# Output projection of the last 14 token tiles: pairs of tiles by seven block products in place of eight

## The chip, the core and the metric

The kernel runs on one core of one Trainium2 chip. TensorE (PE) multiplies, VectorE (DVE), ScalarE (ACT) and GpSimd (POOL) do elementwise work, and the SyncE queue (SP) issues the DMA transfers. The metric is device microseconds for one launch, as a median of runs; the kernel before took 1576.73 us (three runs, 1571.05 to 1579.54).

## The reference

One layer of a hybrid backbone is applied to 128 context tokens and 2048 latent tokens of width 1024. What matters here is the end of the layer:

```
ya = ya.astype(x.dtype) * jax.nn.silu(g_a)
yb = b_gate * _short_conv(c_gate * u_conv, ...) * jax.nn.silu(g_b)
u = jnp.concatenate([ya, yb], axis=-1) @ lp['w_out']        # (tokens x 1024) @ (1024 x 1024)
return x + gate * u, s_final                                # then _rmsnorm(.., final_g)
```

`ya` (channels 0 to 511) comes out of a bidirectional RWKV-7 scan and is the last to be ready; `yb` (channels 512 to 1023) comes out of a short convolution and is ready long before. The output is normalised per token and scaled by `final_g`.

## The kernel before

Phase 1 (to about half of the span) makes the projections and the operands of the scan and spills them to scratch memory. Phase 2 (`phase2`, line 828) runs 17 stages of the scan, each with its masked Gram products (`Gm`, `Fm`, `Qm`), an inverse on GpSimd (`I`, L1103 and L1106), the operators (`E`, L1201, evicted by `Ev`, L1206), the states (`S`, L1232, handed on by `sv`, L1258), the outputs (`y`, L1277 and L1279), and an ending per block of 512 tokens that normalises, gates and stores the mixed channels to scratch (`fw fr fq fm T fy fa`, L1298 to L1339). Stage 15 is the context, stage 16 the last latent block.

Phase 3 (`phase3`, line 1460) is the output projection, mixed into the end of phase 2. It takes 17 tiles of 128 tokens in the order `TILES` (5 to 12, 0, 13 to 16, 1 to 4). Everything is float32 made of two fp32r parts: a high part (a copy on ScalarE) and a low part (the difference, on VectorE). A product of two such numbers is three matmuls: high by high, high by low, low by high. Per tile:

- `cL`, `aL` (or `AL`) load the four conv channel groups and the four scan channel groups of the tile (L1495, 256 KB each); `cH`, `aH` make the high part (L1502, ScalarE), `cD`, `aD` the low part (L1508, VectorE).
- `P` and `B` (L1515 to L1517) are the conv half and the scan half of the product, for each of the two column halves of 512: 4 groups x 3 matmuls = 12 matmuls of 128x512 each, so 48 matmuls per tile and 816 in all. For tiles 5, 6 and 7 (`AHEAD`) the conv half is made ahead (`AP`) and parked by ScalarE (`AE`, L1529).
- `Z` multiplies the sum in PSUM by the gate on VectorE (L1574; with a parked half L1571 and L1572), `G` adds x on GpSimd (L1580; on VectorE for the last tile), `Q` squares and sums on ScalarE (L1588), `ss rt rc` make the inverse root (L1592, L1595, L1598), `fo` scales on VectorE and stores (L1603, L1604), `xL` loads x (L1548).
- The weights are loaded and split once: `CL CH CD` (conv groups, low part on VectorE) and `WL WH WD` (scan groups, low part on GpSimd), L1480 to L1489.

From stage 13 on the order of the work is a list written out by hand, `LATE` (line 778): one word per step, `name@tile` or `name@stage`, run by `main` (line 1398) inside `tc.manual_schedule` for PE, VectorE and ScalarE. The instructions of these three engines stand in the order of the list. GpSimd and the SP queue are ordered by the program's scheduler. `R` opens the first memory of phase 3 (`begin`), `Lo` the rest (`begin_left`, which also loads the gate rows and `final_g`).

Of the kernel before, what the change touches and what calls it, by code (L numbers as in the profile page):

```python
# [827 lines left out]
def phase2(K):  # L828
# [457 lines left out]
    def finish(p, blk, y):  # L1286
# [32 lines left out]
        q = tl([128, 512], "w", 1)  # L1319
# [78 lines left out]
    def main():  # L1398
# [4 lines left out]
        order = tc.manual_schedule(engines={mybir.EngineType.PE, mybir.EngineType.DVE, mybir.EngineType.Activation})  # L1403
# [5 lines left out]
        for word in LATE.split():  # L1409
            n, t = word.split("@")  # L1410
            if n == "R":
                O.pm.close()
                O.r2.close()
                O.r1.close()
                K.last["R"]()
                K.body = NST
            elif n == "Lo":
                for p in (O.p2, O.l1):
                    p.close()
                K.last["Lo"]()  # L1420
            elif "." in t:
# [38 lines left out]
def phase3(K):  # L1460
# [4 lines left out]
    wk, raws, mts, pss, z0, zs, xs, sss = {}, {}, {}, {}, {}, {}, {}, {}  # L1465
    CONV, ATT = (4, 5, 6, 7), (0, 1, 2, 3)
    TILES = [5, 6, 7, 8, 9, 10, 11, 12, 0, 13, 14, 15, 16, 1, 2, 3, 4]
    AHEAD = TILES[:3]
    HALF = [slice(0, 512), slice(512, 1024)]

    def begin():
# [4 lines left out]
        z0[AHEAD[0]] = O.r.tile([128, 1024], F32, name="z0_0")  # L1476
# [42 lines left out]
    def ahead(h):  # L1519
        def f(i):  # L1520
            ps = pss[h, i] = O.pr.tile([128, 512], F32, tag="u", name=f"psa{i}_{h}")
            products(ps, mts["c", i], HALF[h], CONV, True, True)
        return f

    def ahead_out(h):
        def f(i):
            if i not in z0:
                z0[i] = K.spare(5 + len(z0), f"z0_{i}", F32)
            P.copy(z0[i][:, HALF[h]], pss.pop((h, i))[:])  # L1529
# [5 lines left out]
    def begin_left():  # L1535
        O.l = Pool(K, "p3l", "left")
# [40 lines left out]
    def added(h):  # L1577
        def f(i):
            cs = HALF[h]
            (V if i == TILES[-1] else G).tensor_tensor(zs[i][:, cs], zs[i][:, cs], xs[i][:, cs], ALU.add)  # L1580
# [19 lines left out]
    def out(i):  # L1600
        z = zs.pop(i)
        for cs in HALF if i == TILES[-1] else [slice(0, 1024)]:
            V.scalar_tensor_tensor(z[:, cs], z[:, cs], sss[i][:, 0:1], O.fg[:, cs], ALU.mult, ALU.mult)  # L1603
            D(S["y"][i * 128:i * 128 + 128, cs], z[:, cs])  # L1604
# [56 lines left out]
```

## Time and profile before

| | |
|---|---|
| median of 3 runs | 1576.73 us |
| profiled execution | 1576.59 us |
| its span (first to last instruction) | 1574.8 us, granted clock 0.986 |
| busy PE, VectorE, ScalarE, GpSimd | 1491.7, 1158.8, 773.0, 666.4 us |
| 816 products of the output projection | 1364 to 1567 us |

Times in the profile count from the first instruction. The page gives shares over the whole span; this change touches only the end, so the windows from about 1316 us on are read. "Busy" of PE counts pipelined matmuls that overlap; the distance between the starts of two matmuls tells what one costs.

### The profile page before, as it was taken

To read this page: it belongs to the slowest core of one execution; us is meant where nothing else is said; L and a number is where in the kernel's file an instruction comes from. 1 tells how busy PE (TensorE), PEld (TensorE's weight loads), DVE (VectorE), ACT (ScalarE), POOL (GpSimd) and SP (SyncE) were. 2 spreads that over 40 slices of the span, in tenths; PEclk is the share of its full clock that TensorE was granted. 3 is DMA by queue.
4 is the path that set the end of the run, shared out by engine and by line. 5 is a ranking of instruction groups with operands and counts; after the bars stand their busy time and mean duration, and the time that the engine had idled before them with its cause. 6 is when DMAs were issued, how large, how long until landed. Compare 5 with 4: busy or idle time off the path is not lost.

```text
span 1574.8 us, 39408 instructions
## 1 busy us (share of the span) xinstructions
PE 1491.7 (95%) x16180; PEld 1382.8 (88%) x16180; DVE 1158.8 (74%) x1959; ACT 773.0 (49%) x1464; POOL 666.4 (42%) x1026
## 2 busy tenths in 40 slices
PE   5899999999999999999999999999999897899998
PEld 3899989999999999999999997888888786678786
DVE  5999995673999847569995447798998997645533
ACT  4566652342555314136541117887878776523222
POOL 0133330000333572933323605888888887122121
PEclk9999999999999999999999998999999999999999
DMA  9669998653877765538987537566676754636442
GB/s 370 207 189 271 261 268 324 214 203 133 201 230 223 211 234 197 184 106 253 251 244 253 189 124 194 136 178 177 183 209 172 183 155 148 203 116 192 147 142 94
DMA packets 204580, 313.79 MB, mean 199 GB/s; under 512 B 58088, under 2 KB 147560, under 8 KB 190320
## 3 DMA queue, kind: packets, MB, share of 16 engines
q1 hardware_dynamic: 168816, 311.13, 63.3%
q10 hardware_dynamic: 35584, 0.14, 1.4%
q8 instruction: 127, 2.08, 0.6%
q14 instruction: 53, 0.43, 0.1%
HBM read 208.05 MB, written 103.17 MB: 198 GB/s over the span
## 4 chain that ended last, share of the span: by engine, by line
PE 63%; DVE 13%; DMA 8%; POOL 6%; issue 4%; ACT 2%; SPq 1%; ACTq 0%; DVEq 0%; POOLq 0%
PE psE L1201 4%; POOL zt L1106 4%; PE psu L1515 4%; PE psu L1516 4%; PE psu L1517 4%; PE psS L1232 2%; POOL ztmp L1103 2%; PE mmc L182 2%; PE mmc L184 2%; PE mmb L182 2%; PE mmc L183 2%; PE mmb L184 2%; PE mmb L183 2%; PE mmu L182 2%; PE mmu L184 2%
## 5 line engine op out<-in xcount | busy, mean ns | idle before, releaser
L1106 POOL TENSOR_TENSOR zt<-zt,ztmp 128x30 f32<-128x30 f32 (+7 forms) x510 | 213.7, 419 | 39.8
L1103 POOL TENSOR_TENSOR ztmp<-ab,zt 128x60 f32<-128x60 f32 (+7 forms) x255 | 142.2, 558 | 66.9 <-DVE ab L1094 45.4
L1232 PE MATMUL psS<-sv,E 128*64 128x64 f32 x2176 | 103.2, 229 | 13.6 <-DVE sv L1258 9.1
L1232 PEld LDWEIGHTS psS<-sv,E 128*64 128x64 f32 x2176 | 82.4, 138 | 37.8 <-issue 14.5
L410 POOL TENSOR_TENSOR sh<-rawl 128x384 f32<-128x384 f32 (+1 forms) x48 | 46.4, 983 | 151.5 <-ACT rawl L401 151.5
L1580 POOL TENSOR_TENSOR z<-z,x 128x512 f32<-128x512 f32 x32 | 42.7, 1338 | 151.3 <-DVE z L1574 85.9
L1206 DVE TENSOR_TENSOR E<-psE,msk 128x512 f32<-128x512 f32 x136 | 90.9, 684 | 20.8 <-PE psE L1201 19.9
L434 POOL TENSOR_TENSOR hsl<-sq,hsh 128x384 fp32r<-128x384 f32 (+1 forms) x24 | 32.5, 1356 | 129.9 <-ACT hsh L429 129.9
L1187 ACT ACTIVATE stf<-psX 64x512 f32<-64x512 f32 x136 | 80.3, 590 | 13.2 <-PE psX L1183 10.5
L1258 DVE TENSOR_TENSOR sv<-psS,pc 64x128 f32<-64x128 f32 x254 | 64.0, 273 | 22.4 <-PE psS L1232 21.8
L182 PE MATMUL mmg<-h,w 128*128 128x384 f32 (+1 forms) x216 | 70.8, 328 | 0.0
L183 PE MATMUL mmg<-h,w 128*128 128x384 f32 (+1 forms) x216 | 70.7, 327 | 0.0
L184 PE MATMUL mmg<-h,w 128*128 128x384 f32 (+1 forms) x216 | 70.6, 327 | 0.0
L182 PE MATMUL mmb<-h,w 128*128 128x384 f32 (+1 forms) x192 | 62.9, 328 | 5.4 <-ACT w L150 2.8
L184 PE MATMUL mmc<-h,w 128*128 128x384 f32 (+1 forms) x192 | 63.4, 330 | 0.9 <-DVE w L154 0.9
L182 PE MATMUL mmv<-h,w 128*128 128x384 f32 (+1 forms) x192 | 63.1, 328 | 1.1 <-DVE sg L524 1.1
L182 PE MATMUL mmc<-h,w 128*128 128x384 f32 (+1 forms) x192 | 63.5, 331 | 0.2 <-DMA w<-scr_wsp 0.2
L183 PE MATMUL mmc<-h,w 128*128 128x384 f32 (+1 forms) x192 | 63.3, 330 | 0.0
L182 PE MATMUL mmu<-h,w 128*128 128x384 f32 (+1 forms) x192 | 62.7, 326 | 0.0
L184 PE MATMUL mmv<-h,w 128*128 128x384 f32 (+1 forms) x192 | 62.6, 326 | 0.0
L183 PE MATMUL mmb<-h,w 128*128 128x384 f32 (+1 forms) x192 | 62.6, 326 | 0.0
L184 PE MATMUL mmb<-h,w 128*128 128x384 f32 (+1 forms) x192 | 62.6, 326 | 0.0
(316 smaller groups left out, 5069.9 us busy)
## 6 DMA issues: line engine op xcount, KB each, us to landing
w<-scr_wsp SPq DMA_DIRECT2D x68, 1024.0 KB, 6.1
scr_wsp<-w SPq DMA_DIRECT2D x34, 1024.0 KB, 5.2
rr<-scr_ops SPq DMA_DIRECT2D x32, 1024.0 KB, 7.7
scr_ops<-xs SPq DMA_DIRECT2D x160, 192.0 KB, 5.7
wr<-in_win SPq DMA_DIRECT2D x34, 512.0 KB, 8.8
x<-in_x SPq DMA_DIRECT2D x17, 512.0 KB, 3.2
wadas<-in_wada SPq DMA_DIRECT2D x8, 1024.0 KB, 13.6
sv<-scr_vt SPq DMA_DIRECT2D x32, 256.0 KB, 4.1
```

The costliest lines, as they stand in the source:

```text
L182: T.matmul(ps[:, :n], w[:, 0, k], hh[:, 0, k, :n], start=k == 0, stop=False)
L183: T.matmul(ps[:, :n], w[:, 0, k], hh[:, 1, k, :n], start=False, stop=False)
L184: T.matmul(ps[:, :n], w[:, 1, k], hh[:, 0, k, :n], start=False, stop=k == 7)
L1103: G.tensor_tensor(tv, ab[:, j:j + 2, j + 2:32].unsqueeze(1).broadcast_to((128, kn, 2, n)), zt[:, :kn, j:j + 2].unsqueeze(3).broadcast_to(( ...
L1106: G.tensor_tensor(zt[:, :kn, j + 2:32], zt[:, :kn, j + 2:32], tv[:, :, r], ALU.subtract)
L1187: P.activation(g.fs[64:128, :, hd, e::2], g.ps["X"][e][hr_].rearrange("p a (b t) -> p b a t", b=2), AF.Copy, scale=-1.0)
L1201: T.matmul(pe[r, i, hd, :].rearrange("p (b t) -> p b t", b=2), lt[:, b, hd, us.start + k + i], rt[:, :, hd, us.start + k + i], start=True, ...
L1206: V.tensor_tensor(g.E[n][:, k:k + 2].rearrange("p a b c -> p (a b) c"), pe[:].rearrange("p a b c -> p (a b) c"), B.msk[:, ME[g.d]].unsquee ...
L1232: T.matmul(g.sp[i // 4][r, q, hd, :], g.E[n][:, k, hd, r], g.sv[:, u, hd, :], start=True, stop=True)
L1258: V.tensor_tensor(dst, g.sp[i // 4][0:64, q], B.pc[0:64, d, 2 * p:2 * p + 2, c:c + 1].broadcast_to((64, 2, 64)), ALU.mult)
L1515: T.matmul(ps[:], mh[:, n], hi[:, cs], start=start and n == 0, stop=False)
L1516: T.matmul(ps[:], mh[:, n], lo[:, cs], start=False, stop=False)
```

## The change

The order list changes from `R@0` on, and a new word `Tl` at that point ends the ordered block and opens another that also holds GpSimd and SP: from there their instructions, the DMA issues too, stand in the order of the list.

Tiles 5, 6 and 7 (`SINGLE`) stay as they were, 48 matmuls each; the conv half made ahead is kept for tile 5 alone and is cut into words of three matmuls (`A10` and so on). The other 14 tiles go in seven pairs (`TWO`: 8 and 9, 10 and 11, 12 and 0, 13 and 14, 15 and 16, 1 and 2, 3 and 4). A pair is seen as a 2 x 2 block matrix: rows are the two tiles, columns the channel groups `K1` (0, 1, 4, 5) and `K2` (2, 3, 6, 7). The weight is seen as 2 x 2 blocks of `K1`, `K2` by the two column halves. In place of eight block products (96 matmuls) there are seven (`M1` to `M7`, 84 matmuls): four of them take sums of left blocks (`s1` to `s4`), four take sums of right blocks (`t1` to `t4`), and the results are put together by further additions (`EX E2 C11 E3 C22 E4 C12 C21`).

- Per pair: both tiles' mixed channels are loaded by two transfers of 512 KB (`mLa`, `mLb`); four left sums on VectorE (128x512); seven high parts on ScalarE (`H..`) and seven low parts on VectorE (`D..`) in place of four and four.
- Per pair the results: `EX` is a copy on ScalarE, `E2 E3 E4` one VectorE addition each (PSUM plus SBUF), `C11 C22 C12 C21` a VectorE addition and a multiplication by the gate each; before, there were four multiplications (`Z`).
- Once: the four weight groups of each half are loaded again (`vL`, three transfers, 1 MB, four times), 16 right sums on VectorE (`t`), 16 high parts on ScalarE (`tH`), 16 low parts on VectorE (`tD`). The fourth right block overwrites weights that only the single tiles use. The memory for the others is opened by `Lw`, after the last ending of phase 2.
- The additions of x (`G`) stay on GpSimd for 15 tiles; the last two tiles have them on VectorE.
- The last endings of phase 2 (block 0 of p 3) get memory of their own; the states of stage 16, which before lay between the products, come ahead of `Lo`, save the last of them.

```diff
-E010@14 zi@16 ... pre@16 I@16 E110@14 Ev100@14
 ...
-fm@11.1 n@15 Qm0@16 sv11@14 Qe0@16 X0@15 R@0 CL@5 CL@4 S21@14 Xc00@15 T@11.1 sv21@14 S31@14 fy@11.1 Xc10@15
+fm@11.1 n@15 Qm0@16 sv11@14 Qe0@16 X0@15 R@0 Tl@0 y11@13 S21@14 y00@14 CL@5 sv21@14 T@11.1 CL@4 S31@14
 ...
+Ev110@15 U@16 E111@15 WH@0 WL@1 t1@0 sv71@14 Ev111@15 bu@16 E101@15 Ev101@15 E000@15 vL@1 WD@0 E001@15
 ...
+T@14.1 E101@16 Ev001@16 WD@3 AL@5 E100@16 sv61@15 sv71@15 y11@15 fy@14.1 Ev100@16 S00@16 sv00@16 S01@16 WH@2
+sv01@16 E010@16 fa@14.1 S11@16 S10@16 AH@5 Ev010@16 sv10@16 fc@15.1 fw@15.1 AD@5 E011@16 S20@16 sv20@16
 ...
+sv41@16 S51@16 sv50@16 S60@16 A03@5 fy@15.1 Lo@0 aH@5 sv51@16 S61@16 sv60@16 aD@5 fa@15.1 AH@6 AE0@5 S70@16
 ...
+aH@6 fy@16.1 fa@16.1 Lw@0 tH1@0 aD@6 aL@7 Q1@5 tH2@0 P1r@6 tH1@1 AH@7 B0@6 B1@6 tD1@1 tD2@0 tD1@0 tH3@0
+tD3@0 vL@2 aH@7 AD@7 G0@5 tH3@1 Z0@6 aD@7 tD3@1 Z1@6 Q0@5 G0@6 t1@2 t3@2 tH2@1 P0s@7 t2@2 G1@6 ss@5 rt@5
+tH1@2 mLa@0 mLb@0 rc@5 fo@5 tD2@1 tD1@2 P1r@7 vL@3 Q1@6 Ha11@0 Da11@0 s3@0 s1@0 Hs3@0 Ha22@0 s2@0 B1@7 Hs1@0
 ...
+M4@6 rc@1 fo@1 C22@6 G0@3 Q0@3 E4@6 C12@6 G1@4 Q1@4 G1@3 C21@6 Q1@3 ss@3 G0@4 rt@3 rc@3 fo@3 Q0@4 ss@4 rt@4
+rc@4 fo@4
 ...
+            if n == "Tl":
+                order.__exit__(None, None, None)
+                order = tc.manual_schedule(engines={E.PE, E.DVE, E.Activation, E.Pool, E.SP})
+                order.__enter__()
 ...
-            (V if i == TILES[-1] else G).tensor_tensor(zs[i][:, cs], zs[i][:, cs], xs[i][:, cs], ALU.add)
+            (V if i in TILES[-2:] else G).tensor_tensor(zs[i][:, cs], zs[i][:, cs], xs[i][:, cs], ALU.add)
 ...
+    def right_sum(n):
+        def f(j):
+            o = right_raw(n, j)
+            x, y = {1: (right_raw(3, j), o), 3: (right_raw(2, j), o), 2: (o, right_raw(1, j)), 4: (o, right_raw(2, j))}[n]
+            V.tensor_tensor(o, x, y, ALU.subtract)
+        return f
 ...
+    def left_sum(n):
+        def f(q):
 ...
+            x, y, op = dict(s3=("a11", "s1", ALU.subtract), s1=("s1", "a22", ALU.add), s2=("a22", "s3", ALU.subtract),
+                            s4=("a12", "s2", ALU.subtract))[n]
+            V.tensor_tensor(left_raw(n, q), left_raw(x, q), left_raw(y, q), op)
+        return f
 ...
+    def seventh(n):
+        def f(q):
+            c, nm = (q * 7 + ORDER.index(n)) % 4, f"psw{n}_{q}"
+            ps = pss[n, q] = (O.pr if c == 1 else O.pl).tile([128, 512], F32, tag="u", name=nm) if c % 2 else K.bank(nm)
+            mh, ml = lw[LEFT[n], q]
+            for j in range(4):
+                hi, lo = right(n, j)
+                T.matmul(ps[:], mh[:, j], hi, start=j == 0, stop=False)
+                T.matmul(ps[:], mh[:, j], lo, start=False, stop=False)
+                T.matmul(ps[:], ml[:, j], hi, start=False, stop=j == 3)
+        return f
 ...
+    def plus(n, src, dst, gate=False):
+        def f(q):
+            z, gb = part(q, *dst)
+            V.tensor_tensor(z, pss[n, q][:], part(q, *src)[0], ALU.add)
+            if gate:
+                V.tensor_tensor(z, z, gb, ALU.mult)
+        return f
```

More of the change, by code (lines that the diff above doesn't have):

```diff
@@ L1420, in main @@
                 K.last["Lo"]()
+            elif n == "Lw":
+                O.l0.close()
+                K.last["Lw"]()
             elif "." in t:
@@ L1429, in main, with small, bank @@
         O.pS.close()
-        for p in (O.l0, O.rI, O.r0):
+        for p in (O.rI, O.r0):
             p.close()
-    K.early, K.main, K.spare = early, main, spare
+    def small(tag, name, dt=F32):
+        return (O.rI if tag in ("zt", "dg") else O.r0).tile([128, 512], dt, tag=tag, name=name, bufs=2 if tag == "zt" else 1)
+    def bank(name):
+        return O.pS.tile([128, 512], F32, tag="S", name=name)
+    K.early, K.main, K.spare, K.small, K.bank = early, main, spare, small, bank
 def layout2(I):
@@ L1517, in products, with ahead @@
             T.matmul(ps[:], ml[:, n], hi[:, cs], start=False, stop=stop and n == 3)
-    def ahead(h):
+    def ahead(h, n):
         def f(i):
-            ps = pss[h, i] = O.pr.tile([128, 512], F32, tag="u", name=f"psa{i}_{h}")
-            products(ps, mts["c", i], HALF[h], CONV, True, True)
+            if n == 0:
+                pss["a", h, i] = O.pr.tile([128, 512], F32, tag="u", name=f"psa{i}_{h}")
+            ps, (mh, ml), (hi, lo), cs = pss["a", h, i], mts["c", i], wk[CONV[n]], HALF[h]
+            T.matmul(ps[:], mh[:, n], hi[:, cs], start=n == 0, stop=False)
+            T.matmul(ps[:], mh[:, n], lo[:, cs], start=False, stop=False)
+            T.matmul(ps[:], ml[:, n], hi[:, cs], start=False, stop=n == 3)
         return f
@@ L1526, in f @@
         def f(i):
[L1527 to L1529 removed]
+            P.copy(z0[i][:, HALF[h]], pss.pop(("a", h, i))[:])
         return f
@@ L1535, in begin_left @@
     def begin_left():
-        O.l = Pool(K, "p3l", "left")
+        O.l = Pool(K, "p3l", "right")
         O.pl = Pool(K, "p3pl", "left", 2, PSUM)
@@ L1601, in out, with two_ways @@
         z = zs.pop(i)
-        for cs in HALF if i == TILES[-1] else [slice(0, 1024)]:
+        for cs in HALF if i in TILES[-2:] else [slice(0, 1024)]:
             V.scalar_tensor_tensor(z[:, cs], z[:, cs], sss[i][:, 0:1], O.fg[:, cs], ALU.mult, ALU.mult)
             D(S["y"][i * 128:i * 128 + 128, cs], z[:, cs])
+    def two_ways():
+        O.w = Pool(K, "p3w", "left")
+        for n in range(1, 4):
+            tw[n] = [[O.w.tile([128, 512], F32R, name=f"tw{n}{a}{j}") if (n, j, a) != (1, 0, "h") else K.small("dg", "tw1h0", F32R) for a in "hl"] for j in range(4)]
+        tw[4] = [[w[:, HALF[1]] for w in wk[k]] for k in K1]
@@ new lines, in again, with right_raw @@
+    def again(j):
+        vr = raws["v", j] = K.spare(6 + j % 2, f"wa{j}", F32), K.small("zt", f"wb{j}"), K.small(("Q00", "Q01", "Q10", "Q11")[j], f"wc{j}")
+        a, b = [slice(k * 128, k * 128 + 128) for k in (K1[j], K2[j])]
+        D(vr[0][:], A["wout"][a, :])
+        D(vr[1][:], A["wout"][b, HALF[1]])
+        D(vr[2][:], A["wout"][b, HALF[0]])
+    def right_raw(n, j):
+        ab, b22, b21 = raws["v", j]
+        return {1: ab[:, HALF[0]], 2: b22[:], 3: ab[:, HALF[1]], 4: b21[:]}[n]
@@ new lines, in part, with first_out, f @@
+    def part(q, r, h):
+        i = TWO[q][r]
+        return zs[i][:, HALF[h]], O.gb[:, 0 if i else 1, HALF[h]]
+    def first_out(q):
+        for t, i in zip((0, 1), TWO[q]):
+            zs[i] = K.spare(6 + t, f"zw{i}", F32) if q % 2 else tl([128, 1024], "z", i)
+        P.copy(part(q, 1, 0)[0], pss[1, q][:])
+    def plus(n, src, dst, gate=False):
+        def f(q):
+            z, gb = part(q, *dst)
+            V.tensor_tensor(z, pss[n, q][:], part(q, *src)[0], ALU.add)
+            if gate:
+                V.tensor_tensor(z, z, gb, ALU.mult)
+        return f
@@ L1613, in phase3 @@
     for h in range(2):
-        K.last.update({f"AP{h}": ahead(h), f"AE{h}": ahead_out(h), f"P{h}r": conv_part(h, "pr"), f"P{h}l": conv_part(h, "pl"),
+        K.last.update({f"A{h}{n}": ahead(h, n) for n in range(4)})
+        K.last.update({f"AE{h}": ahead_out(h), f"P{h}r": conv_part(h, "pr"), f"P{h}l": conv_part(h, "pl"), f"P{h}s": conv_part(h, "pS"),
                        f"B{h}": att_part(h), f"Z{h}": gated(h), f"G{h}": added(h), f"Q{h}": squares(h)})
+    for n in range(1, 5):
+        K.last.update({f"t{n}": right_sum(n), f"tH{n}": right_high(n), f"tD{n}": right_low(n), f"s{n}": left_sum(f"s{n}")})
+    for n in LEFT.values():
+        K.last.update({f"H{n}": left_high(n), f"D{n}": left_low(n)})
+    for n in range(1, 8):
+        K.last[f"M{n}"] = seventh(n)
+    K.last.update(EX=first_out, E2=plus(6, (1, 0), (0, 1)), C11=plus(2, (1, 0), (0, 0), True), E3=plus(7, (0, 1), (1, 0)),
+                  C22=plus(5, (1, 0), (1, 1), True), E4=plus(5, (0, 1), (0, 1)), C12=plus(3, (0, 1), (0, 1), True), C21=plus(4, (1, 0), (1, 0), True))
+    K.last.update(Lw=lambda _=0: two_ways(), vL=again, mLa=both_load(0), mLb=both_load(1))
 def layout3(I):
```

148 lines of the change are left out of this document (98 added, 50 removed).

## The prediction

> **What bounds the kernel now.** I first read the windows of the end, where the change lies: per stretch, busy time of PE, PEld, VectorE, ScalarE and GpSimd (instructions in brackets), granted clock, DMA share, GB/s.
>
> ```profile
> span 1574.8 us, 39408 instructions
> ...
> 1316.20:1364.20 48.00, 36.13 (x718) 30.49 (x717) 31.79 (x60) 31.77 (x50) 19.75 (x26) 0.93 0.56 167
> 1364.20:1405.40 41.20, 37.47 (x171) 29.40 (x169) 17.65 (x29) 11.32 (x25) 5.63 (x5) 0.92 0.51 158
> 1405.40:1449.00 43.60, 43.60 (x224) 34.71 (x223) 29.83 (x50) 11.59 (x31) 10.83 (x8) 1.00 0.54 176
> 1449.00:1567.40 118.40, 118.34 (x552) 95.25 (x550) 49.31 (x84) 29.86 (x73) 26.38 (x20) 1.00 0.40 135
> 1567.40:1574.80 7.40, 0.00 (x0) 0.00 (x0) 3.10 (x6) 1.02 (x3) 0.00 (x0) 0.63 0.20 72
> 1316.20:1574.80 258.60, 235.55 (x1657) 189.84 (x1656) 131.69 (x227) 85.56 (x180) 62.58 (x59) 0.96 0.47 149
> ```
>
> From 1405 to 1567 us TensorE never stops, and VectorE is free more than half of the time (118.4 - 49.3 us in the longest stretch). So the products set the end, and a product less is time won as long as VectorE, which takes the additions, does not become the bound. The 48 us before 1364 are bound otherwise, by the scan's chain: TensorE idles 12 us there. What a product costs is the distance between starts; the timeline of PE has two starts 48 matmuls apart:
>
> ```profile
> 1545.21 0.39 PE L1515 MATMUL psu<-woh,mhc 128*128 128x512 f32 x1
> ...
> 1556.19 0.39 PE L1515 MATMUL psu<-woh,mhc 128*128 128x512 f32 x1
> ```
>
> (1556.19 - 1545.21) / 48 = 0.229 us, not the 0.39 us shown as duration.
>
> **The change part by part. Products.** Seven pairs lose 12 matmuls each: 84 x 0.229 = 19.2 us. This is the most that the smaller count can give; a pair goes from 96 x 0.229 = 22.0 to 19.2 us.
>
> **VectorE.** Its cost is again the distance to the next start, in the timeline of VectorE:
>
> ```profile
> 1451.53 0.69 DVE L1574 TENSOR_TENSOR z<-psu,gb 128x512 f32<-128x512 f32 x1 [2.90 <-DMA out_y<-z]
> 1452.14 0.68 DVE L1508 TENSOR_TENSOR mlc<-mxc,mhc 128x512 fp32r<-128x512 f32 x1
> ...
> 1412.61 0.69 DVE L1571 TENSOR_TENSOR z<-psu,z 128x512 f32<-128x512 f32 x1
> 1413.33 0.69 DVE L1572 TENSOR_TENSOR z<-z,gb 128x512 f32<-128x512 f32 x1
> 1413.94 0.69 DVE L1571 TENSOR_TENSOR z<-psu,z 128x512 f32<-128x512 f32 x1
> ...
> 1458.13 1.28 DVE L1603 SCALAR_TENSOR_TENSOR z<-z,ss,fg 128x1024 f32<-128x1024 f32 x1
> 1459.35 0.28 DVE L1258 TENSOR_TENSOR sv<-psS,pc 64x128 f32<-64x128 f32 x1
> ```
>
> A 128x512 operation costs 0.61 us, 0.72 where the next needs its result (1412.61 to 1413.33), and the scaling of a whole tile 1.22. An addition with its gate multiplication is 0.72 + 0.61 = 1.33. No row shows the sums `s` and `t`; they are two-input operations of L1508's size, bounds 0.61 and 0.72, and I take 0.64. Added per pair: four sums 2.6, three low parts 1.8, `E2 E3 E4` 1.9, and four times 1.33 in place of 0.61 for the results, 2.9: 9.2 us, 64 us for seven pairs. Once: 16 sums and 16 low parts, 10.2 + 9.8 = 20 us. Two additions of x come over from GpSimd (+1.4), and tiles 6 and 7 no longer add a parked half (-2.8). Together about 82 us more. The small operations are in the groups by line (behind the bar their busy time and the mean ns of one):
>
> ```profile
> L1592 DVE TENSOR_TENSOR ss<-ss 128x1 f32<-128x1 f32 x17 | 4.6, 270 | 21.3 <-ACT sq L1588 21.2
> L1598 DVE RECIPROCAL ss<-ss 128x1 f32<-128x1 f32 x17 | 2.7, 161 | 4.3 <-ACT ss L1595 4.3
> ```
>
> Per pair VectorE then has 4 x 0.64 + 7 x 0.61 + 3 x 0.64 + 4 x 1.33 + 2 x 1.22 for `fo` + 2 x (0.27 + 0.16) for the small ones = 17.4 us, against 19.2 us of TensorE: 90%, with no contention yet.
>
> **Contention with GpSimd.** The cover of VectorE's new work is thin, so its delays count. These rows show it, GpSimd's addition `G` ahead of what VectorE did meanwhile:
>
> ```profile
> 1414.24 1.29 POOL L1580 TENSOR_TENSOR z<-z,x 128x512 f32<-128x512 f32 x1 [11.51 <-DVE z L1572]
> ...
> 1414.66 1.42 DVE L1572 TENSOR_TENSOR z<-z,gb 128x512 f32<-128x512 f32 x1
> ...
> 1485.34 1.28 POOL L1580 TENSOR_TENSOR z<-z,x 128x512 f32<-128x512 f32 x1 [2.28 <-DVE ss L1598]
> ...
> 1485.38 2.33 DVE L1603 SCALAR_TENSOR_TENSOR z<-z,ss,fg 128x1024 f32<-128x1024 f32 x1
> ...
> 1396.57 1.29 POOL L1580 TENSOR_TENSOR z<-z,x 128x512 f32<-128x512 f32 x1 [9.28 <-DVE z L1572]
> ...
> 1396.81 0.69 DVE L1571 TENSOR_TENSOR z<-psu,z 128x512 f32<-128x512 f32 x1 [0.32 <-PE psu L1517]
> 1397.53 0.88 DVE L1572 TENSOR_TENSOR z<-z,gb 128x512 f32<-128x512 f32 x1
> ```
>
> A VectorE operation with both inputs in SBUF that falls into a `G` waits until it is over: 1.42 in place of 0.69, 2.33 in place of 1.28; L1571, with one input in PSUM, keeps 0.69. The three delays here are 0.73, 1.05 and 0.19 us, mean 0.66; VectorE was often idle then. Afterwards a two-input operation is nearly always due (sums, low parts, gate, `fo`). 30 `G` stay on GpSimd; the delay of each lies between 0 (it falls on PSUM readers) and its whole 1.29 us. I take 0.72, a little over the mean seen: 21.6 us in all, bounds 0 and 38.7. The Trainium skill, "SBUF — State Buffer", section "Who interferes with whom", states it as a rule: a VectorE instruction with two SBUF inputs contends with a GpSimd instruction that reads SBUF, and the loser "**fully blocks** (not throttle)". By that rule the trace agrees, 2.33 against 1.28 us; read strictly with VectorE always due, it is the third rival below.
>
> **The start of the end, to `Lo`.** Its length comes from the scan's chain. In the timeline of PE, the first states of stage 16, and a step of the chain of states:
>
> ```profile
> 1322.88 0.45 PE L1232 MATMUL psS<-sv,E 128*64 128x64 f32 x8 [0.59 <-DVE sv L1258]
> 1323.72 0.45 PE L1232 MATMUL psS<-sv,E 128*64 128x64 f32 x8 [0.39 <-DVE sv L1258]
> ...
> 1362.08 0.63 PE L1232 MATMUL psS<-sv,E 128*64 128x64 f32 x16
> ```
>
> A step is 0.84 us. Stage 16 starts at 1362.1, and the new order runs seven steps of it ahead of `Lo` (before, they lay between products at no wait): 5.9 us, plus some 3 us for three more sums on VectorE (1.9) and six more DMA issues ahead on SP. I put `Lo` at 1371 in place of 1364, bounds 1367 and 1380. That is not lost: the 24 products made ahead for tile 5 (5.5 us) and stage 16's states lie in the idle places of this stretch.
>
> **From `Lo` on.** TensorE: 732 - 24 = 708 products x 0.229 = 162, with the last states and transposes 165 us. VectorE: by the word list with the prices above, 41 of its 204 us lie before `Lo` and 163 after; with contention 184 us. The left parts run ahead, but only as far as their single buffers allow, and `M1` of the first pair stands behind the right parts, so VectorE, which is short of time from `Lo` on, holds TensorE there. Its own waits I take as 3 us (between 0 and the fifth rival's share). At the end stay the last squares, root and store. The end before, in VectorE's timeline:
>
> ```profile
> 1567.38 0.69 DVE L1574 TENSOR_TENSOR z<-psu,gb 128x512 f32<-128x512 f32 x1 [4.07 <-PE psu L1517]
> ...
> 1570.37 1.41 DVE L1603 SCALAR_TENSOR_TENSOR z<-z,ss,fg 128x512 f32<-128x512 f32 x2
> ```
>
> 1574.8 - 1571.8 = 3.0 us for the last transfer and about 2 for squares and root: 5 us. High parts, `EX` and roots on ScalarE add 21 us to the 86 of 258.6 it is busy: hidden. Sum: 1371 + 184 + 3 + 5 = 1563 us of span. The execution took 1.8 us more than its span (1576.59 against 1574.8), so 1565 us; it stands 0.1 us from the median.
>
> **The re-throttled clock** is a risk in every stall that VectorE causes; the timeline of PE after a wait:
>
> ```profile
> 1382.94 0.80 PE L1515 MATMUL psa<-woh,mhc 128*128 128x512 f32 x1 [3.73 <-ACT mhc L1502]
> ...
> 1388.22 0.48 PE L1515 MATMUL psa<-woh,mhc 128*128 128x512 f32 x1
> ```
>
> Twelve matmuls in 5.28 us in place of 2.75: a stall of 3.7 us costs another 2.5. It matters only where TensorE is the bound, so it is not in the sum. The Trainium skill, "TensorE: Matmul & The Clock Gate", section "What's actually happening", puts the rule at one idle window of about 3.4 us; by that rule shorter waits, spread, would cost nothing more, and the trace agrees with its one case.
>
> **The rivals.** *Forecast, VectorE sets the end*: 1565, chance 0.44, own range 1557 to 1573 (delay per `G` 0.45 to 1.0).
>
> *TensorE stays the bound* (0.18): `Lo` 1371 + 165 + about 12 for the last pair's results (`C21`, two additions of x, two `fo`, the store) = 1548, time 1550. It holds if `G` costs VectorE under 0.2 us each. For it: the additions that read PSUM (7 of about 25 per pair) are free of it, and eight PSUM banks of results let TensorE run ahead. Against: 90% without contention.
>
> *Every `G` blocks VectorE for its whole 1.29 us* (0.14): 1371 + 163 + 38.7 + 8 = 1581, time 1582. For it: the row of 2.33 us. Against: 0.19.
>
> *Loads late* (0.10): the weights read again are 4 MB, and SP now runs in fixed order, each store ahead of the loads behind it. The chain of waits and SP's waits show both before:
>
> ```profile
> 1372.00 10.16 DMA mxc<-scr_mixT
> ...
> SPq L1604 <- DVE z L1603: 45.9, 15, 10.2
> ```
>
> A wait like that 10.2 us once more: 1575. Against: the loads of tile 5's and 6's conv half stand ahead of `Lo`'s burst now.
>
> *VectorE's list stops in order* (0.14), the rival on the other side: 82 us of new work stand in one queue, and a sum that waits for a load, or a result for a product, holds all low parts behind it, and TensorE with them. In the tightest stretch before, VectorE was busy 89% (103.5 of 116.2):
>
> ```profile
> 1200.00:1316.20 116.20, 105.99 (x2738) 93.97 (x2730) 103.50 (x213) 90.41 (x171) 99.90 (x219) 1.00 0.62 162
> ```
>
> At that share 184 / 0.89 = 207, 1371 + 207 + 5 = 1583; with the whole 1.29 us 201.5 / 0.89 = 226, 1602. I take 1586 span, time 1588. It is slower than before once the share falls under 184 / (1574.8 - 1371 - 5) = 93%.
>
> **How the numbers follow.** A measurement of this kernel can tell about 0.5% from no change: faster is under 1568.8, slower over 1584.6. Forecast 0.44: 0.33 faster, 0.11 same. TensorE 0.18 faster. Whole lock 0.14: 0.105 same, 0.035 slower. Loads 0.10: 0.02 faster, 0.07 same, 0.01 slower. Stops 0.14: 0.035 same, 0.105 slower. Together faster 0.53, same 0.32, slower 0.15. The range runs from the TensorE case with 3 us to spare, 1547, to 1587, which leaves half of the stops out.
>
> **What would show it.** Right: 732 products of 0.229 us; VectorE busy over 90% from `Lo` to the end; TensorE's idle after `Lo` released by VectorE (low parts, `E`, `C`); two-input VectorE operations well over 0.69 us in the mean, PSUM readers at 0.69; `Lo`'s gate loads issued near 1371. Wrong: TensorE without gaps from the first pair on (second case), idle time released by DMA (fourth), or VectorE with idle of its own above 7% (fifth). A start to `Lo` beyond 1380 would break the sum at its first term.

## The result, and the profile after

The changed kernel takes 1561.17 us (median of 7 runs, 1558.68 to 1566.3), the kernel before beside it 1576.73 us (7 runs, 1571.05 to 1580.72). The ratio is 0.9909, 95% interval 0.9883 to 0.9936: faster by 0.9%. The forecast was 1565, with a range of 1547 to 1587. The profiled execution took 1559.04 us with a span of 1557.3; its numbers are compared with those of the profiled execution before.

The windows of the end, with the columns of the prediction (us, PE, PEld, VectorE, ScalarE, GpSimd, granted clock, DMA share, GB/s); the cuts lie at the issue of the gate loads of `Lo` (1365.3), the first block product (1406.1), and behind the last product (1549; it ends at 1546.8). In the stretches of the result and the experiments, "from `Lo`" means from the issue of these gate loads:

```profile
PE 1471.6 (95%) x16096; PEld 1365.6 (88%) x16096; DVE 1249.0 (80%) x2088; ACT 793.2 (51%) x1504; POOL 677.5 (44%) x1024
...
1365.30:1406.10 40.80, 38.55 (x223) 30.11 (x222) 37.23 (x65) 14.58 (x31) 6.01 (x4) 0.96 0.72 227
1406.10:1425.00 18.90, 18.90 (x84) 15.40 (x83) 17.99 (x31) 9.64 (x22) 5.12 (x2) 1.00 0.62 218
1425.00:1549.00 124.00, 118.22 (x507) 94.32 (x505) 121.56 (x179) 47.12 (x112) 37.37 (x24) 1.00 0.44 144
1549.00:1557.30 8.30, 0.00 (x0) 0.00 (x0) 4.70 (x11) 1.82 (x6) 0.00 (x0) 0.53 0.34 126
1365.30:1557.30 192.00, 175.67 (x810) 139.84 (x808) 181.48 (x283) 73.16 (x168) 48.50 (x30) 0.97 0.51 168
1313.90:1557.30 243.40, 216.55 (x1572) 173.77 (x1572) 221.77 (x357) 105.25 (x219) 67.64 (x60) 0.96 0.54 176
```

TensorE has 84 matmuls less than before, and VectorE 90 us more. In the long stretch of the pairs VectorE is busy 121.56 of 124 us, 98%; before it was busy 49.3 of 118.4. TensorE, which had no gap there before, now waits 3.6 us between 1425 and the end of the last product. What released TensorE after each of its waits from `Lo` to the last product (total us, times, longest):

```profile
PE psw L1733 <- DVE mls L1709: 3.6, 5, 1.1
PE psu L1543 <- DVE mla L1534: 2.3, 1, 2.3
```

Both rows name VectorE, the first with a low part of the pairs (`D`), the second with one of a single tile, and none names a DMA. VectorE's groups from `Lo` to the end (operation, output and inputs, count | busy us, mean ns of one | idle time before, with its releaser):

```profile
L1748 DVE TENSOR_TENSOR z<-psw,z 128x512 f32<-128x512 f32 x28 | 18.8, 682 | 0.6 <-PE psw L1733 0.4
L1748 DVE TENSOR_TENSOR zw<-psw,zw 128x512 f32<-128x512 f32 x21 | 14.1, 682 | 0.2
L1709 DVE TENSOR_TENSOR mls<-ma,mhs 128x512 fp32r<-128x512 f32 x14 | 12.7, 916 | 0.1
L1709 DVE TENSOR_TENSOR mla<-ma,mha 128x512 fp32r<-128x512 f32 x14 | 12.2, 874 | 0.0
...
L1632 DVE SCALAR_TENSOR_TENSOR zw<-zw,ss,fg 128x1024 f32<-128x1024 f32 x6 | 8.7, 1456 | 0.3
L1693 DVE TENSOR_TENSOR ma<-ma,mb 128x512 f32<-128x512 f32 x7 | 6.8, 965 | 0.1
```

The additions that read PSUM (L1748) keep their 682 ns. The operations with both inputs in SBUF are longer in the mean: low parts 874 and 916, a left sum 965, the scaling of a whole tile 1456 against 1280 where it runs alone. That is the pattern that the prediction named for contention with GpSimd.

Last, the instructions that place both stretches in time, of the kernel before and then of the changed one (duration minimum, median, maximum; start of the first and the last). The first load of the output weights is the point `R` from which the program differs:

```profile
L1480 SPq DMA_DIRECT2D woraw<-in_wout x8: 328/336/1488, 1316.3 to 1352.0; - x8
L1542 SPq DMA_DIRECT2D gb<-scr_gate x2: 423/440/457, 1367.6 to 1368.1; - x2
```

```profile
L1506 SPq DMA_DIRECT2D woraw<-in_wout x8: 327/382/538, 1313.9 to 1350.0; - x8
L1570 SPq DMA_DIRECT2D gb<-scr_gate x2: 422/460/497, 1365.3 to 1365.8; - x2
```

From `R` to the end it was 1574.8 - 1316.3 = 258.5 us and is 243.4: 15.1 us less. Another 2.4 us of the shorter span lie ahead of `R`, where both programs are the same; `R` lay between 1310.6 and 1325.1 in the kernels of this study. Stretches are therefore compared below, beside the medians; each comes from the one profiled execution of its kernel.

### The profile page after: what moved, and what is told of

Same layout as the page of the kernel before. It is cut to its first block, busy times and chain, and to the rows that moved or that the text cites. A ratio compares the mean times of both kernels' runs of the same rounds, so it can differ in the third digit from the quotient of the medians.

```text
span 1557.3 us, 39384 instructions
## 1 busy us (share of the span) xinstructions
PE 1471.6 (95%) x16096; PEld 1365.6 (88%) x16096; DVE 1249.0 (80%) x2088; ACT 793.2 (51%) x1504; POOL 677.5 (44%) x1024
## 4 chain that ended last, share of the span: by engine, by line
PE 52%; DVE 16%; POOL 14%; DMA 8%; issue 7%; ACT 2%; SPq 1%; ACTq 0%; DVEq 0%; POOLq 0%
POOL zt L1113 8%; POOL ztmp L1110 5%; PE mmb L182 2%; PE mmb L184 2%; PE mmb L183 2%; PE psE L1208 2%; PE mmc L184 2%; PE mmgb L183 2%; PE mmgb L184 2%; PE mmgb L182 2%; PE mmu L182 2%; PE mmu L184 2%; PE mmc L182 2%; PE mmu L183 2%; PE mmc L183 2%
## 5 line engine op out<-in xcount | busy, mean ns | idle before, releaser
L1113 POOL TENSOR_TENSOR zt<-zt,ztmp 128x30 f32<-128x30 f32 (+7 forms) x510 | 218.4, 428 | 40.0
L1609 POOL TENSOR_TENSOR z<-z,x 128x512 f32<-128x512 f32 x18 | 28.9, 1612 | 92.6 <-DVE z L1750 39.1
L184 PE MATMUL mmc<-h,w 128*128 128x384 f32 (+1 forms) x192 | 62.7, 327 | 0.9 <-DVE w L154 0.9
L184 PE MATMUL mmk<-h,w 128*128 128x384 f32 (+1 forms) x184 | 60.3, 328 | 2.6 <-DVE w L154 2.6
L182 PE MATMUL mmc<-h,w 128*128 128x384 f32 (+1 forms) x192 | 62.6, 326 | 0.0
## 6 DMA issues: line engine op xcount, KB each, us to landing
scr_ops<-xs SPq DMA_DIRECT2D x160, 192.0 KB, 6.0
```

The source lines that it names most:

```text
L182: T.matmul(ps[:, :n], w[:, 0, k], hh[:, 0, k, :n], start=k == 0, stop=False)
L184: T.matmul(ps[:, :n], w[:, 1, k], hh[:, 0, k, :n], start=False, stop=k == 7)
L1113: G.tensor_tensor(zt[:, :kn, j + 2:32], zt[:, :kn, j + 2:32], tv[:, :, r], ALU.subtract)
```

## The experiments

The theory, V: from `Lo` on VectorE sets the end, with its own work and some 0.7 us for each addition of x on GpSimd. Rivals: TensorE still sets it (T); the loads or the order of VectorE's list do (L). Beside them stood the question of what the fixed order of GpSimd and SP does by itself. All ratios are to the kernel before, run beside on the same chip; not all experiments ran on one chip.

### A third of the block products' matmuls left out

```diff
                 T.matmul(ps[:], mh[:, j], hi, start=j == 0, stop=False)
-                T.matmul(ps[:], mh[:, j], lo, start=False, stop=False)
-                T.matmul(ps[:], ml[:, j], hi, start=False, stop=j == 3)
+                T.matmul(ps[:], mh[:, j], lo, start=False, stop=j == 3)
```

> The changed kernel with the third matmul of every block product (low part of the left by high part of the right) left out in the seven pairs: 196 matmuls x 0.229 = 45 us of TensorE less; all of VectorE's work stays. Theory V (VectorE sets the end of the pairs; it was busy 139.6 of the 142.9 us from the first block product on): time stays near 1561, at most the 6 us of TensorE's own idle places less, 1555 to 1561. Rival P (the products still set the end): 20 to 45 us less, 1541 or below.

1557.85 us, ratio 0.9881 (0.986 to 0.9903). From `Lo` to the end, in the windows' columns:

```profile
1361.70:1551.60 189.90, 142.42 (x614) 108.40 (x612) 180.25 (x282) 73.18 (x168) 47.77 (x30) 0.89 0.53 170
```

196 matmuls are gone, 196 x 0.229 = 45 us of TensorE's work, and the stretch is 189.9 in place of 192.0 us. VectorE's busy time is the same. TensorE was not what set the end; T falls.

### GpSimd's additions cut short

```diff
-            (V if i in TILES[-2:] else G).tensor_tensor(zs[i][:, cs], zs[i][:, cs], xs[i][:, cs], ALU.add)
+            if i in TILES[-2:]:
+                V.tensor_tensor(zs[i][:, cs], zs[i][:, cs], xs[i][:, cs], ALU.add)
+            else:
+                cs = slice(cs.start, cs.start + 16)
+                G.tensor_tensor(zs[i][:, cs], zs[i][:, cs], xs[i][:, cs], ALU.add)
```

> The changed kernel with GpSimd's addition of x cut to 16 of the 512 columns (the other columns get no x): 30 operations of 1.29 us become short, all waits and orders stay. Theory V with the lock: VectorE's two-input operations fall back to 0.69 us in the mean, it gets back some 15 to 20 us (30 x 0.5 to 0.7) and TensorE becomes the bound: 6 to 10 us less, 1551 to 1555. Rival P: no change, 1561. Theory V without contention: no change either, but with VectorE's long two-input operations still there.

The kernel leaves x out of the other 496 columns of each half. 1554.13 us, ratio 0.9859 (0.9832 to 0.9886). The window from `Lo` to the end, and then VectorE's groups in it:

```profile
1369.60:1552.30 182.70, 172.65 (x810) 139.18 (x808) 162.77 (x283) 72.89 (x168) 16.34 (x30) 0.98 0.54 177
```

```profile
L1752 DVE TENSOR_TENSOR z<-psw,z 128x512 f32<-128x512 f32 x28 | 18.9, 684 | 3.4 <-PE psw L1737 3.4
...
L1713 DVE TENSOR_TENSOR mls<-ma,mhs 128x512 fp32r<-128x512 f32 x14 | 9.6, 683 | 3.1 <-ACT mhs L1708 3.0
L1713 DVE TENSOR_TENSOR mla<-ma,mha 128x512 fp32r<-128x512 f32 x14 | 9.5, 686 | 0.2 <-ACT mha L1708 0.2
...
L1636 DVE SCALAR_TENSOR_TENSOR zw<-zw,ss,fg 128x1024 f32<-128x1024 f32 x6 | 7.7, 1281 | 0.3
```

With the same 283 instructions VectorE is busy 162.77 in place of 181.48 us. The low parts are back at 683 to 686 ns and the scaling at 1281. So the excess was GpSimd's doing: 18.7 us, 18.7 / 30 = 0.62 us for each addition. The stretch shrinks only by 9.3 us, because TensorE then sets it: VectorE now waits for products (the rows' last column), and TensorE has this one wait in the stretch:

```profile
PE psu L1543 <- DVE mla L1534: 1.2, 1, 1.2
```

V is shown, and also how near the next bound lies.

### All additions of x on VectorE

```diff
-            (V if i in TILES[-2:] else G).tensor_tensor(zs[i][:, cs], zs[i][:, cs], xs[i][:, cs], ALU.add)
+            V.tensor_tensor(zs[i][:, cs], zs[i][:, cs], xs[i][:, cs], ALU.add)
```

> The changed kernel with all additions of x on VectorE: 30 operations of 0.61 to 0.72 us more on it (18 to 22 us), none on GpSimd, so nothing blocks it. Theory V with the lock at 0.5 to 0.7 us per addition: about the same, 1559 to 1569. Theory V without a price for the lock: 18 us more, 1576 to 1582. Rival P: no change as long as VectorE has room, 1561.

1556.83 us, ratio 0.988 (0.9861 to 0.9899): faster than any of the three expectations. It was run a second time later, on the same chip as the six pairs further down:

> Seven pairs, all additions of x on VectorE, a second time, beside the six pairs on the same chip. If what was measured before holds: 1553 to 1560, 0.985 to 0.990 of the kernel before, and a stretch of 187 to 190 us from the gate loads to the end. If it was the chance of one chip: the changed kernel's 1561 or over, 192 us.

1555.2 us, ratio 0.9878 (0.9858 to 0.9898). The window from `Lo` to the end, in the first of the two:

```profile
1364.60:1553.00 188.40, 174.71 (x810) 138.56 (x808) 180.49 (x313) 73.11 (x168) 0.00 (x0) 0.99 0.52 172
```

VectorE has 30 instructions more and is busy no longer: 180.49 against 181.48 us. Doing an addition costs it (180.49 - 162.77) / 30 = 0.59 us, and letting GpSimd do it cost 0.62. The stretch is 188.4 us, and 188.8 the second time, against 192.0. Both measured ratios lie under the changed kernel's, but their intervals overlap with its own. That this version beats the kernel before is shown; that it beats the changed kernel is likely by the stretches (two executions of it, one of the changed kernel), but not shown.

### Left sums on GpSimd

```diff
-            V.tensor_tensor(left_raw(n, q), left_raw(x, q), left_raw(y, q), op)
+            G.tensor_tensor(left_raw(n, q), left_raw(x, q), left_raw(y, q), op)
```

> The changed kernel with the four left sums of each pair on GpSimd: 28 operations of 0.61 us less on VectorE (17 us), 28 of 1.29 us more on GpSimd. Theory V with the lock: each new GpSimd operation blocks VectorE for 0.5 to 0.7 us, which eats the 17 us, and the left parts come later: 1559 to 1572. Theory V without the lock: VectorE gets 17 us, TensorE becomes the bound, 1551 to 1555. Rival P: 1561.

1571.25 us, ratio 0.9976 (0.9953 to 0.9998). The window from `Lo` to the end, and VectorE's groups:

```profile
1369.70:1570.20 200.50, 177.06 (x810) 139.44 (x808) 183.86 (x254) 73.09 (x168) 88.16 (x58) 0.97 0.49 161
```

```profile
L1709 DVE TENSOR_TENSOR mls<-ma,mhs 128x512 fp32r<-128x512 f32 x14 | 15.9, 1144 | 3.0 <-ACT mhs L1704 2.1 <-issue 0.8
...
L1709 DVE TENSOR_TENSOR mls<-mb,mhs 128x512 fp32r<-128x512 f32 x7 | 8.1, 1152 | 0.0
```

28 sums left VectorE, 21.2 us of its busy time in the changed kernel, and it is busier than before they left. Low parts that took 916 and 839 ns take 1144 and 1152. Each moved sum cost VectorE (183.86 - 181.48 + 21.2) / 28 = 0.84 us of blocked time. The stretch grew by 8.5 us, and with it most of the gain was gone.

### An eighth product

`M7` is made twice over in each pair, as 84 matmuls more, for nothing but their time.

```diff
-            for j in range(4):
+            for j in [0, 1, 2, 3] * (2 if n == 7 else 1):
```

> The changed kernel with the seventh block product of each pair made twice (the second starts the sum afresh, the result is the same): 84 matmuls x 0.229 = 19.2 us more on TensorE, nothing else. Theory V: TensorE goes from 175.7 busy us behind Lo to 195, past VectorE's 181.5 in 192: 6 to 14 us more, 1567 to 1575. Rival P (products still set the end): the whole 19 us, 1580.

1573.73 us, ratio 0.9992 (0.9975 to 1.0009). From `Lo` to the end:

```profile
1367.20:1572.40 205.20, 193.96 (x894) 155.76 (x892) 182.19 (x283) 73.19 (x168) 48.70 (x30) 0.98 0.47 158
```

19.2 us were added to TensorE, and the stretch grew by 13.2. Some 6 us were free, as much as TensorE had waited for VectorE (3.6 + 2.3); beyond that TensorE sets the end, busy 194 of 205 us. So at seven products the two engines stand some 6 us apart. With all of the change's edits but as many matmuls as before, the kernel is as fast as before.

### The fixed order alone

The kernel before, with the new word `Tl` and nothing else: from `R` on GpSimd's work and SP's DMA issues stand in the order of the old list.

```diff
+            if n == "Tl":
+                order.__exit__(None, None, None)
+                order = tc.manual_schedule(engines={E.PE, E.DVE, E.Activation, E.Pool, E.SP})
+                order.__enter__()
```

> The kernel before with one part of the change alone: from R on, GpSimd and the DMA issues also stand in the order of the list; products, list and steps stay those of before. If the gain is that of the products and of the states moved off them: no change, 1572 to 1581. Rival, the fixed order brings a part of the gain: 1570 or less. Rival, the order holds loads behind stores: 1584 or more.

1568.06 us, ratio 0.997 (0.9953 to 0.9986): 4.7 us faster, as the second of the three expectations had it. Where, shows the stretch of the 72 products that are made ahead (`psa`), first in the kernel before and then with the order fixed:

```profile
1364.20:1390.90 26.70, 22.97 (x102) 17.83 (x101) 10.09 (x18) 5.74 (x11) 1.38 (x2) 0.87 0.57 180
```

```profile
1359.00:1379.10 20.10, 20.10 (x102) 16.09 (x101) 10.11 (x18) 5.84 (x11) 1.40 (x2) 1.00 0.78 236
...
1312.60:1563.00 250.40, 232.64 (x1656) 187.50 (x1654) 133.29 (x227) 85.53 (x180) 63.36 (x66) 0.98 0.48 154
```

The same 102 matmuls take 26.7 us before, with TensorE idle for 3.7 and at a clock of 0.87, and 20.1 us without a gap at 1.00. What is gone is the wait for the 10.16 us load of `mxc` that the prediction quoted, and the slower clock behind it; these are 6.6 us, and 1.5 us more lie between `R` and these products (47.9 us before, 46.4 now). From `R` to the end it is 250.4 in place of 258.5 us. Of the 15.1 us that the whole change saved from `R` on, 8.1 are thus there with the order alone, in one execution of each; by the ratios it is 4.7 us (0.3%) of the change's 14.3 (0.91%). What is left for the seven products and all that comes with them is 250.4 - 243.4 = 7.0 us in the stretches and 9.6 us by the ratios. That the two parts add up is taken for granted here: no run has the changed list without the fixed order.

### Six pairs

If VectorE sets the end by a few us over TensorE, a pair less should be the better balance: it gives TensorE 2.7 us and takes 7 to 9 from VectorE. Tiles 8 and 9 were made singly again, ahead of six pairs, in a list written by hand around them; in the second kernel all additions of x lie on VectorE as well.

```diff
-tH1@2 mLa@0 mLb@0 rc@5 fo@5 tD2@1 tD1@2 P1r@7 vL@3 Q1@6 Ha11@0 Da11@0 s3@0 s1@0 Hs3@0 Ha22@0 s2@0 B1@7 Hs1@0
 ...
+cL@8 rc@5 fo@5 tD2@1 tD1@2 P1r@7 vL@3 Q1@6 cH@8 cD@8 aL@8 B1@7 tH3@2 Q0@6 t1@3 B0@7 P0l@8 aH@8
 ...
+P1s@9 tH2@3 tD2@3 rc@7 Z0@8 fo@7 mLa@1 B1@9 G1@8 Ha11@1 xL@9 G0@8 Da11@1 mLb@1 B0@9 Q1@8 Ha12@1 tH4@1
```

> The changed kernel with tiles 8 and 9 taken singly again, with 48 matmuls each, ahead of the pairs; six pairs. TensorE 12 matmuls = 2.7 us more, VectorE some 9 us less. Theory V: VectorE's 181.5 us behind Lo become 172, TensorE's 175.7 become 178 and are the bound: 3 to 8 us less, 1553 to 1558. Rival P: 2.7 us more, 1564. The list around the two tiles is written by hand, so up to 3 us may be lost there in either case.

> As the run with six pairs, and all additions of x on VectorE. Theory V: VectorE about 180.5 - 9 = 172 us behind Lo without a lock, TensorE 178: 1551 to 1557, 4 to 10 us less than the changed kernel and a little less than the kernel with seven pairs and these additions on VectorE. Rival P: 1564.

1574.08 us, ratio 0.9994 (0.9976 to 1.0013), and 1567.75 us, ratio 0.9968 (0.9947 to 0.9989): both missed. The busy times came out as meant (VectorE 174 and 172 us after `Lo`), but both engines stood still between the single tiles and the first pair, here in the second kernel:

```profile
1430.00:1450.00 20.00, 14.11 (x53) 10.64 (x52) 14.77 (x27) 7.84 (x18) 0.00 (x0) 0.83 0.41 122
```

The first pair's load stood late in the list. So it was issued earlier, and the first pair's left parts were spread among the words of tiles 8 and 9:

```diff
-cH@9 cD@9 aL@9 fo@6 B0@8 Q1@7
+cH@9 cD@9 aL@9 mLa@1 fo@6 B0@8 Q1@7
 ...
+xL@8 P0r@9 aH@9 Ha11@1 aD@9 mLb@1 Da11@1 Q0@7 ss@7 rt@7 Z1@8 Ha12@1 s3@1 Hs3@1 P1s@9
```

> Tiles 8 and 9 are made singly again ahead of six pairs, all additions of x lie on VectorE, and the first pair's loads, left parts, sums and low parts stand as early in the list as their buffers allow, so that they are worked on while TensorE multiplies the single tiles; in the run of six pairs before this one they stood behind them and both engines stood still between 1425 and 1455. VectorE sets the end: VectorE is busy about 172 us after the gate loads and TensorE 179; with the hole of some 10 us gone, the stretch from the gate loads to the end is 184 to 190 us, against 188.4 with seven pairs and 198.5 with the hole; time 1552 to 1560. Position of loads was not the cause: the hole stays somewhere else, the stretch is 196 to 200 us, time 1565 to 1570.

1566.83 us, ratio 0.9959 (0.9938 to 0.9981), a stretch of 201.8 us: the hole stayed. Its windows, and in the fences behind them TensorE's, ScalarE's and VectorE's timelines there (start, duration, operation, in brackets the wait before it and its releaser):

```profile
1430.00:1450.00 20.00, 14.07 (x48) 10.99 (x49) 16.35 (x28) 8.06 (x19) 0.00 (x0) 0.74 0.37 123
1470.00:1530.00 60.00, 59.79 (x258) 47.80 (x257) 59.14 (x100) 24.00 (x57) 0.00 (x0) 1.00 0.48 158
```

```profile
1430.98 0.40 PE L1727 MATMUL psw<-tw2l,mhs 128*128 128x512 f32 x1
1436.66 0.79 PE L1728 MATMUL psw<-tw2h,mls 128*128 128x512 f32 x1 [5.29 <-DVE mls L1704]
1437.25 0.63 PE L1726 MATMUL psw<-tw2h,mhs 128*128 128x512 f32 x1
1437.68 0.63 PE L1727 MATMUL psw<-tw2l,mhs 128*128 128x512 f32 x1
...
1442.80 0.42 PE L1727 MATMUL psw<-wol,mha 128*128 128x512 f32 x1
```

```profile
1426.95 0.62 ACT L1699 CAST mha<-ma 128x512 fp32r<-128x512 f32 x1 [6.47 <-PE psu L1537]
1427.48 0.61 ACT L1699 CAST mhs<-ma 128x512 fp32r<-128x512 f32 x1
```

```profile
1428.64 0.69 DVE L1662 TENSOR_TENSOR tw2l<-wb,tw2h 128x512 fp32r<-128x512 f32 x1 [4.27 <-ACT tw2h L1656]
...
1435.92 0.69 DVE L1704 TENSOR_TENSOR mls<-s2r,mhs 128x512 fp32r<-128x512 f32 x1
```

`Ha12` now stood early in ScalarE's queue and waited 6.47 us for the memory of a high part that the products of a single tile still read. The high parts of the sums were queued behind it. VectorE stood still behind ScalarE for 4.27 us and then had its list to work off, so that the low part of a sum that TensorE waited for came only at 1435.92; TensorE stood for 5.29 us. That is rival L, made by the hand-written order: the mechanism that the prediction feared for the changed kernel, at another place. The second window says what the pairs are like once they run: TensorE and VectorE both all but without a gap (59.8 and 59.1 of 60 us). Whether six pairs in a good order beat seven is left open; no list of mine was free of the hole.

## Why the prediction was right, and where it was not

- **What bounds it.** That VectorE takes over from TensorE as the bound was right, and shown from four sides: less work for TensorE moves little (the first experiment), less for VectorE moves much, work taken off VectorE onto GpSimd comes back as blocked time, and work added to TensorE is free for some 6 us only.
- **The products.** 84 matmuls less, as said. They are not worth their 19.2 us: what is left for the products and all that comes with them is 7 us in the stretches (9.6 by the ratios), since VectorE stopped the gain.
- **Contention.** 0.72 us for each `G` was predicted, 21.6 in all; measured 0.62, 18.7 in all. The mean of three delays seen (0.66) would have been the better choice. The rival in which each `G` blocks for its whole 1.29 us is refuted by the same number. The Trainium skill, "SBUF — State Buffer", section "Who interferes with whom", has the rule that the loser is fully blocked; the runs agree, in that a scaling of 1.28 us took 2.32 while a `G` ran (last section), but the mean cost of a `G` was half its length. That much of the other half falls on VectorE's operations that read PSUM fits the groups (682 ns), but was not measured by itself; and GpSimd was delayed too, its 30 additions taking 48.5 us in place of 30 x 1.29 = 38.7.
- **`Lo` itself.** The prediction's 1371 is the place of `Lo` in the lists, and it took the gate loads to be issued at the same time. They were issued at 1365.3: SP, in its own list, had come to `Lo` before VectorE had. So the sign "gate loads issued near 1371" did not come true, and it was a bad mark: SP's own waits move it too, so that it stood behind `Lo`'s place on VectorE before (1367.6) and ahead of it afterwards. VectorE's first operation behind `Lo`, in the kernel before, with the order alone and in the changed kernel:

```profile
1363.80 0.28 DVE L1258 TENSOR_TENSOR sv<-psS,pc 64x128 f32<-64x128 f32 x1
```

```profile
1358.62 0.27 DVE L1258 TENSOR_TENSOR sv<-psS,pc 64x128 f32<-64x128 f32 x1
```

```profile
1371.12 0.52 DVE L1265 TENSOR_TENSOR sv<-psS,pc 64x128 f32<-64x128 f32 x2
```

  By this place 1371 was hit, with luck: from `R` on it is 47.5 us before and 57.2 in the changed kernel, 9.7 us more and not 7, and `R` itself came 2.4 us earlier by chance. The order alone gives 46.0, so the added work may have cost some 11 us.
- **From `Lo` to the end: the term that was off.** 184 + 3 + 5 = 192 us was predicted from that place. It took 186.2. The windows from there to the end, of the changed kernel and of the one with GpSimd's additions cut short:

```profile
1371.10:1557.30 186.20, 169.87 (x751) 135.60 (x747) 175.85 (x268) 72.54 (x167) 48.50 (x30) 0.97 0.50 166
```

```profile
1375.40:1552.30 176.90, 166.85 (x751) 134.95 (x747) 157.15 (x268) 72.27 (x167) 16.34 (x30) 0.98 0.53 174
```

  VectorE was busy 175.85 us, 8 less than the 184, and idle 10.4 in place of 3 + 5, most of it ahead of the pairs and at the end. Its own work, put at 163 us from distances between starts, was 157.15, 6 us less; contention was 3 us less. Which of the prices were too high was not measured. That 192.0 us also lie between the issue of the gate loads and the end is chance: 5.6 us of VectorE's work in that stretch belong ahead of `Lo`.
- **The total.** The sum was 1563 us of span, and the profiled execution has 1557.3. The 5.8 us between them are VectorE's 8 too many, less 2.4 of idle time too few; the longer way to `Lo` and the earlier `R` cancel.
- **The fixed order** appears in the prediction only as a danger (each store ahead of the loads behind it). It had the 10.16 us load and the slower clock quoted in it, and did not ask what the same order does for them.
- **TensorE after `Lo`** was put at 165 us and was busy 169.9 (first row above). 708 x 0.229 = 162 was fair; 3 us for the rest, the last states and transposes and the slower clock ahead of the pairs, was some 5 us too little. It did no harm to the time, as VectorE stood above it, but it made the margin 6 us and not 19, and the rival in which TensorE stays the bound would have come to some 1554, as with the additions cut short, and not to 1550.
- **Loads late.** ScalarE waited 21.1 us for the pairs' loads, but no wait of TensorE and none of VectorE over 1.0 us was released by a load. Right to leave it out.
- **VectorE's list stops in order.** A share of 89% was the price of that rival; it was 98% in the pairs and 94% from `Lo` to the end. Here the list was good enough for VectorE hardly to stop. The experiment with six pairs shows the mechanism to be real.
- **The clock.** The longest of TensorE's waits in the pairs was 1.1 us, and the granted clock stayed at 1.00. Behind the 5.29 us of the six pairs the matmuls stood 0.43 us apart in place of 0.229 for some 5.5 us. The Trainium skill, "TensorE: Matmul & The Clock Gate", section "What's actually happening", gives an idle window of about 3.4 us as the limit, and by it, the prediction said, shorter waits would cost nothing more. The runs do not bear that out. In the changed kernel, ahead of the pairs, TensorE waited 2.25 us, and three matmuls later the next eight stood 0.43 us apart, 3.0 us long:

```profile
1388.30 0.50 PE L1543 MATMUL psu<-woh,mla 128*128 128x512 f32 x1 [2.25 <-DVE mla L1534]
...
1389.13 0.63 PE L1543 MATMUL psu<-woh,mla 128*128 128x512 f32 x1
1389.56 0.63 PE L1541 MATMUL psu<-woh,mha 128*128 128x512 f32 x1
```

  With the eighth product a wait of 1.87 us did the same, and with the left sums on GpSimd one of 1.78 us did, while one of 2.35 us in that same run did not. No single length of a wait is the limit here.

## What to carry to other kernels

When a change takes work from one engine by giving more to another, price the second engine's whole new list from distances between starts and add what its neighbours do to it; here that sum (184 us) came out 5% above what was measured (175.85 us), while the work saved (19.2 us) was worth a third to a half of itself. Then measure from the point that the sum was counted from: an engine with a list of its own, here SP, passes the same word of the list at another time. Near a balance of two engines every further saving on one alone is cut off after a few us, so ask where the next bound lies before spending effort on it. And price each edit alone, the side edits too: fixing the order of GpSimd and of the DMA issues, by itself, gave a third of the gain by the ratios and half of it in the stretches.

## What the runs showed of the hardware

Moving a 128x512 addition from a full VectorE to GpSimd did not help it here, where other VectorE operations read two inputs from SBUF: doing it cost VectorE 0.59 us, leaving it to GpSimd 0.62 us of blocked time, and 0.84 us for the left sums, many of which GpSimd ran right behind one another. GpSimd was no cheap helper here: leaving it the work cost VectorE as much as doing it. GpSimd pays too: its addition, 1.29 us in the prediction's rows, took over 1.6 us in the mean beside a full VectorE, as its groups from `Lo` to the end in the changed kernel show:

```profile
L1609 POOL TENSOR_TENSOR z<-z,x 128x512 f32<-128x512 f32 x18 | 28.9, 1612 | 92.6 <-DVE z L1750 39.1 <-DVE z L1603 21.5 <-DVE yss L1325 20.7
L1609 POOL TENSOR_TENSOR zw<-zw,x 128x512 f32<-128x512 f32 x12 | 19.6, 1642 | 35.2 <-DVE zw L1750 11.1 <-DMA x<-in_x 8.1 <-issue 6.0
```

Both delays at once, in the timeline of the changed kernel: an addition on GpSimd takes 1.56 us, and the scaling that VectorE starts meanwhile 2.32:

```profile
1443.29 1.56 POOL L1609 TENSOR_TENSOR zw<-zw,x 128x512 f32<-128x512 f32 x1 [3.54 <-DMA x<-in_x]
1443.62 2.32 DVE L1632 SCALAR_TENSOR_TENSOR z<-z,ss,fg 128x1024 f32<-128x1024 f32 x1
```
